# The low part of every fourth half piece of weights: from a subtraction on VectorE to an accumulating DMA

## The chip, the cores and the metric

The kernel runs on one core of a Trainium2 chip. The metric is the time of one execution on the device in microseconds (us). The engines are called TensorE (PE in the profile; PEld is its loading of stationary operands), VectorE (DVE), ScalarE (ACT), GpSimd (POOL) and SyncE (SP), which issues most of the DMAs.

## What is computed

Two transformer blocks follow each other on 256 tokens of 1024 columns, all in float32:

```
x = first_block(x, ...)        # u = rms_norm(h); z = u @ w_in; block-wise attention beside a gated
                               # recurrence; h += merged @ w_out;
                               # u = rms_norm(h); g, up = u @ w_gate_up; h += (silu(g) * up) @ w_down
for i in range(2):             # second block, two layers
    x += 0.5 * swiglu(rmsnorm(x, ffn1_norm[i]), w_gate, w_up, w_down)
    proj = rmsnorm(x, mix_norm[i]) @ w_in[i];  mkv = rmsnorm(mem, mem_norm[i]) @ w_mem_kv[i]
    x += concat([self_attention, memory_attention]) @ w_out[i]
    x += 0.5 * swiglu(rmsnorm(x, ffn2_norm[i]), w_gate, w_up, w_down)
```

## The kernel before

All weights are one stream of 227 pieces of 128 x 2048 float32 numbers (1 MB each). `load_to` has SP load a piece into one of three `raw` buffers. A piece is two half pieces of 128 x 1024. `split_to` makes two float32r operands of each: ScalarE casts it to the high part `wh` (line 204) and VectorE subtracts this from the original to get the low part `wl` (line 205), 512 columns at a time. There are eight buffers for `wh` and eight for `wl`, so a half piece takes over the buffers of the one eight places before it in the stream, and both wait until TensorE has read that one for the last time. In the program a split is asked for four half pieces ahead of the use (`SPLIT_AHEAD`).

An activation, which is the stationary operand, is split in the same way (`uh`, `ul`; `hh`, `hl`), and a product is three matmuls (`mm3`): high by high, high activation by `wl`, low activation by `wh`. Each half piece is used twice, for the first 128 tokens (t = 0) and for the second (t = 1).

Five feed-forwards (`ffn_body`) make up most of the time. In step j of 11 the stages are `gu(0, j)`, `dn(0, j-1)`, `gu(1, j)`, `dn(1, j-1)`. A `gu` uses four half pieces, in 24 matmuls; a `dn` uses two, in 12. The result of a `gu` goes through a tanh on ScalarE (`th`, line 356) and two instructions on VectorE (lines 357 and 359, to `hid`), and then TensorE transposes it in the next stage but one (line 154, `trbank<-cst,hid`), after six of its matmuls. Norms use a power on GpSimd (`power`, line 261, to `r` and `fac`).

TensorE's order is written out by hand: `Order` keeps a clock and places the small products of attention and recurrence beside the stream. The order on the other engines is a list scheduler's; `crit()` raises the priority of what stands under it. Each engine runs its own list in order.

Of the kernel before, what the change touches and what calls it, by code (L numbers as in the profile page):

```python
# [13 lines left out]
ALU = mybir.AluOpType  # L14
# [16 lines left out]
# the second block's distances on the clock of Order, by layer and then by group of heads (MEM: the memory's) and half of  # L31
# the tokens: projection to normalised heads, scores to the next group's, scores to normalised probabilities
# [5 lines left out]
# columns of the constants  # L38
C_ID, C_INV = 0, 128
C_N = 160  # L40
# columns of the constants of the first block
D_TRI, D_ONE, D_COS, D_SIN, D_CAUS, D_MLM, D_CHK = 0, 128, 256, 384, 512, 640, 768
D_N = 896
# columns of the per-partition parameters
# [5 lines left out]
# columns of the parameters that lie along the free dimension  # L50
# [4 lines left out]
class Ready:  # L55
    """When the operands of a later product can be expected, on the clock of Order."""
# [5 lines left out]
class Order:  # L62
    """Places the work beside the stream of large products in TensorE's program order.

    A task is a generator that emits instructions and yields what it waits for: a distance on the clock, or a list of
    Ready. The clock advances by the cost of the products emitted.
    """
# [30 lines left out]
    def until(self, *events):  # L98
        """Lets tasks go on until the events are ready."""
        self.run()  # L100
        while self._due(events) > self.now:
            nxt = min([self._due(w) for _, w in self.tasks] + [self._due(events)])
            assert nxt < math.inf
            self.now = max(self.now, nxt)
            self.run()
# [8 lines left out]
def kernel(  # L114
# [66 lines left out]
    # ScalarE's tables are loaded before the first operands are there  # L181
# [25 lines left out]
    def split_to(n):  # L207
        """Splits the first n half pieces."""
        while stream["split"] < min(n, 2 * NP):
# [5 lines left out]
            for s in range(0, 1024, SPLIT_W):  # L215
                split(hi[:, s:s + SPLIT_W], lo[:, s:s + SPLIT_W], r[:, 1024 * m + s:1024 * m + s + SPLIT_W])
# [14 lines left out]
    def lin(u, pieces, k0=0):  # L231
        """[tokens, 512] = u @ the pieces, each of four k tiles by 512 columns."""
# [13 lines left out]
    def lin_both(us, pieces):  # L246
        """lin for both halves of the tokens, which take turns."""
# [15 lines left out]
    def row_rstd(src, prescale=None):  # L263
        """rstd of the rows of src, or of src times prescale."""
# [24 lines left out]
    def put_T(u, k0, n, src, gains=None, gain1=None, keep=None):  # L289
        """u[:, k0:k0+n] = the n blocks of 128 columns of src, transposed, times gains, in two parts."""  # L290
# [18 lines left out]
    def boundary(t, src, gains, wait=1.4, keep=None, after=None):  # L309
        """The transposed operand of the next products: src times gains."""  # L310
# [108 lines left out]
    def scores(mix, qT, kT, t, n, st, mask=None, bias=None):  # L419
        """Softmax numerators and sums of four heads; qT, kT: [128, 2 pairs, tokens].  # L420

        mask: an operand and its identity, added by TensorE to the last 128 keys; bias: [128, 4 heads, n].
        """
# [33 lines left out]
    def probs_T(dst, p, n):  # L457
        """dst = the transposed blocks of p, [128, heads, keys], by head and by block of keys."""
# [10 lines left out]
    def heads_out(u, k0, st, v):  # L469
        """u[:, k0:k0 + 2] = the transposed sums over keys of four heads, in two parts; v(kb, head): values."""  # L470
# [9 lines left out]
    # =========================== first block ===========================  # L480
    def first_mix(p0):
        with tc.tile_pool(name="mix1", bufs=1, reuse_waits="tile") as mix:
# [25 lines left out]
            # the input in transposed form, and the gates of the recurrence from it  # L508
            def chain(*parts):
                """A task of parts, each a function and the time after it."""  # L510
# [77 lines left out]
            # -- recurrence --  # L588
# [110 lines left out]
            # -- attention --  # L699
# [706 lines left out]
```

## Time and profile before

| | |
|---|---|
| time, median of 2 executions | 1406.24 us (1406.09 and 1406.39) |
| span of the profiled execution, first to last instruction | 1404.3 us |
| TensorE busy | 1384.1 us, 99% |
| VectorE busy | 921.4 us, 66% |
| ScalarE busy | 766.8 us, 55% |
| GpSimd busy | 57.8 us, 4% |
| granted TensorE clock | 1.000 (2.4 GHz) over the span |
| DMA | 246.59 MB, mean 176 GB/s |

The profiled execution's own time is not listed apart from the two times; the start and the end that lie around its span are the difference, about 1.9 us. Busy time leaves out the issuing of DMAs and waiting for semaphores. Matmuls overlap each other, so the rows give them some 0.39 us each while one starts every 0.23 us. In the stretch of the feed-forward that the rows show, from 294.3 on, one step takes 17.06 us.

### The profile page before, as it was taken

Reading aid. Unit: us, or ns where it says so; the run is one execution under the profiler, and the core shown is the slowest. Engines: PE = TensorE matmul, PEld = TensorE weight load, DVE = VectorE, ACT = ScalarE, POOL = GpSimd, SP = SyncE. Lnnn points to the kernel's source line nnn. Section 1 sums busy time; section 2 is a strip of 40 time slices with the busy share of each in tenths; the row PEclk is TensorE's granted clock in tenths of the full one; section 3 lists DMA queues with packets and bytes.
Section 4 is the critical chain, followed back from the end, with each engine's and each line's share of the span. In section 5 each row is a group of like instructions: output and inputs, shape, how many; then the busy total and the mean of one; then the engine's idle time right before and its main releaser. Section 6 shows DMA issues by size and latency. Waiting matters only on the chain.

```text
span 1404.3 us, 18083 instructions
## 1 busy us (share of the span) xinstructions
PE 1384.1 (99%) x6598; PEld 1124.1 (80%) x6598; DVE 921.4 (66%) x1839; ACT 766.8 (55%) x1577; POOL 57.8 (4%) x59
## 2 busy tenths in 40 slices
PE   8999999999999999999999999999999989999998
PEld 6777888888888888877888888888888767888887
DVE  7866587555585575768575665755756787755554
ACT  6556555444474454668565544644545567544442
POOL 0000000000010000022000000000000121000000
PEclk9999999999999999999999999999999999999999
DMA  7534546554546454554255555555454532455540
GB/s 293 180 122 149 180 144 240 191 192 183 180 171 220 180 180 180 175 196 155 91 184 192 194 186 196 210 189 195 166 203 155 182 121 96 172 185 196 191 180 30
DMA packets 37081, 246.59 MB, mean 176 GB/s; under 512 B 4736, under 2 KB 5760, under 8 KB 8064
## 3 DMA queue, kind: packets, MB, share of 16 engines
q1 hardware_dynamic: 35568, 243.09, 48.4%
q10 hardware_dynamic: 1424, 2.34, 0.5%
q8 instruction: 52, 0.85, 0.2%
q14 instruction: 37, 0.30, 0.1%
HBM read 244.37 MB, written 1.05 MB: 175 GB/s over the span
## 4 chain that ended last, share of the span: by engine, by line
PE 90%; DVE 6%; POOL 2%; ACT 1%; issue 1%; DMA 0%; SPq 0%; DVEq 0%; POOLq 0%; ACTq 0%
PE bank L149 86%; PE trbank L154 4%; POOL fac L261 2%; DVE wl L205 2%; DVE ms L942 1%; ACT p L443 1%; DVE nm L441 1%; DVE z L946 1%; DMA h<-in_x_dram 0%; DVE p L453 0%; DVE p L439 0%; DVE z L1004 0%; DVE p L1041 0%; DVE z L1006 0%; DVE z L1007 0%
## 5 line engine op out<-in xcount | busy, mean ns | idle before, releaser
L205 DVE TENSOR_TENSOR wl<-raw,wh 128x512 fp32r<-128x512 f32 x908 | 583.7, 687 | 193.1 <-ACT wh L204 190.3
L204 ACT CAST wh<-raw 128x512 fp32r<-128x512 f32 x908 | 518.2, 619 | 238.4 <-PE bank L149 228.8
L149 PE MATMUL bank<-wh,uh 128*128 128x512 f32 x1248 | 505.8, 405 | 0.0
L149 PE MATMUL bank<-wh,ul 128*128 128x512 f32 x1248 | 490.4, 393 | 0.0
L149 PE MATMUL bank<-wl,uh 128*128 128x512 f32 x1248 | 487.5, 391 | 0.0
L149 PEld LDWEIGHTS bank<-wh,ul 128*128 128x128 f32 x1248 | 234.5, 188 | 52.8
L149 PEld LDWEIGHTS bank<-wl,uh 128*128 128x128 f32 x1248 | 235.3, 189 | 44.7 <-DVE wl L205 0.3
L149 PEld LDWEIGHTS bank<-wh,uh 128*128 128x128 f32 x1248 | 235.1, 188 | 44.6 <-issue 1.9
L149 PE MATMUL bank<-wh,hh 128*128 128x512 f32 x440 | 173.0, 393 | 0.0
L149 PE MATMUL bank<-wl,hh 128*128 128x512 f32 x440 | 172.4, 392 | 0.0
L149 PE MATMUL bank<-wh,hl 128*128 128x512 f32 x440 | 172.4, 392 | 0.0
L356 ACT ACTIVATE th<-bank,rs 128x256 f32<-128x256 f32 x110 | 52.2, 475 | 189.1 <-PE bank L149 188.8
L357 DVE SCALAR_TENSOR_TENSOR th<-th,bank 128x256 f32<-128x256 f32 x110 | 46.3, 421 | 166.3 <-ACT th L356 166.3
L149 PEld LDWEIGHTS bank<-wl,hh 128*128 128x128 f32 x440 | 82.7, 188 | 18.3
L149 PEld LDWEIGHTS bank<-wh,hl 128*128 128x128 f32 x440 | 82.6, 188 | 18.0
L149 PEld LDWEIGHTS bank<-wh,hh 128*128 128x128 f32 x440 | 82.8, 188 | 17.5
L204 ACT CAST hh<-trbank 128x256 fp32r<-128x256 f32 x110 | 40.6, 369 | 49.9 <-PE trbank L154 49.9
L261 POOL TENSOR_TENSOR r<-ms,mhalf 128x1 f32<-128x1 f32 x22 | 18.4, 837 | 908.9 <-DVE ms L271 908.9
L359 DVE SCALAR_TENSOR_TENSOR hid<-bank,rs,th 128x256 f32<-128x256 f32 x110 | 53.2, 484 | 3.5
L205 DVE TENSOR_TENSOR hl<-trbank,hh 128x256 fp32r<-128x256 f32 x110 | 46.1, 419 | 10.4 <-ACT hh L204 10.3
L261 POOL TENSOR_TENSOR fac<-ms,mhalf 128x4 f32<-128x4 f32 (+2 forms) x26 | 38.1, 1464 | 246.6 <-DVE ms L943 139.1
L154 PEld LDWEIGHTS trbank<-cst,hid 128*128 128x128 f32 x220 | 30.4, 139 | 14.6
(223 smaller groups left out, 947.2 us busy)
## 6 DMA issues: line engine op xcount, KB each, us to landing
raw<-in_weights_dram SPq DMA_DIRECT2D x226, 1024.0 KB, 4.9
mem<-in_mem_dram ACTq DMA_DIRECT2D x4, 512.0 KB, 4.5
Tb<-in_rel_dram SPq DMA_DIRECT2D x3, 512.0 KB, 5.9
h<-in_x_dram SPq DMA_DIRECT2D x4, 256.0 KB, 3.9
raw<-in_weights_dram SPq DMA_DIRECT2D x2, 512.0 KB, 7.1
gf<-in_rows_dram SPq DMA_DIRECT2D x1, 512.0 KB, 4.2
out_dram<-h SPq DMA_DIRECT2D x2, 256.0 KB, 2.0
out_dram<-h SPq DMA_DIRECT2D x4, 128.0 KB, 1.8
```

The costliest lines, as they stand in the source:

```text
L149: pe.matmul(out=out, lhsT=lhsT, rhs=rhs, start=start, stop=stop)
L154: pe.transpose(out=out, in_=in_, identity=ident if identity is None else identity)
L204: act.copy(out=hi, in_=src)
L205: dve.tensor_tensor(out=lo, in0=src, in1=hi.bitcast(F32), op=ALU.subtract)
L261: pool.tensor_tensor(out=dst, in0=src, in1=mhalf[:, 0:n], op=ALU.pow)
L356: act.activation(out=th, in_=acc[:, 0:256], func=AF.Tanh, scale=rh[t])
L357: dve.scalar_tensor_tensor(out=th, in0=th, scalar=1.0, in1=acc[:, 0:256], op0=ALU.add, op1=ALU.mult)
L359: dve.scalar_tensor_tensor(out=hd, in0=acc[:, 256:512], scalar=r2[t], in1=th, op0=ALU.mult, op1=ALU.mult)
L441: dve.tensor_reduce(out=nm, in_=s, axis=AX.X, op=ALU.max, negate=True)
L443: act.activation(out=p[:, j, a, 0:n], in_=s[:, j], func=AF.Exp, bias=nm[:, j:j + 1], accum_out=sums[:, j, a:a + 1])
L942: dve.tensor_reduce(out=ms, in_=sq, axis=AX.X, op=ALU.add)
L946: dve.tensor_tensor(out=v, in0=v, in1=fac.unsqueeze(2).to_broadcast([128, n, w]), op=ALU.mult)
```

## The change

From piece 8 on, every fourth half piece (the second half of each odd piece, 109 of 454) is split in another way. ScalarE writes the negated source, rounded to float32r, into `wl` in one instruction of 1024 columns; GpSimd issues a DMA that adds the source itself onto it, out of the same `raw` buffer; ScalarE casts the source to `wh` in one more instruction of 1024 columns. VectorE has no part in it. Comments are dropped elsewhere in the file, which moves line numbers by 7 behind this place (204 and 205 stay).

```diff
@@ split_to
             hi = wp.tile([128, 1024], FR, tag="wh", bufs=W_BUFS, name="wh")
             lo = wp.tile([128, 1024], FR, tag="wl", bufs=W_BUFS, name="wl")
-            for s in range(0, 1024, SPLIT_W):
-                split(hi[:, s:s + SPLIT_W], lo[:, s:s + SPLIT_W], r[:, 1024 * m + s:1024 * m + s + SPLIT_W])
+            if i >= 8 and (2 * i + m) % 4 == 3:
+
+                src = r[:, 1024 * m:1024 * m + 1024]
+                act.activation(out=lo, in_=src, func=AF.Copy, scale=-1.0)
+                pool.dma_start(out=lo, in_=src, accum_op=ALU.add)
+                act.copy(out=hi, in_=src)
+            else:
+                for s in range(0, 1024, SPLIT_W):
+                    split(hi[:, s:s + SPLIT_W], lo[:, s:s + SPLIT_W], r[:, 1024 * m + s:1024 * m + s + SPLIT_W])
```

In the whole program ScalarE has 690 casts of 128x512 and 109 of 128x1024 to `wh` where it had 908 of 128x512, and 109 negations of 128x1024; VectorE has 690 subtractions to `wl` where it had 908; GpSimd has 109 DMAs that it did not have. TensorE's order and SP's are the same.

The first place is ScalarE's list in the feed-forward of the first block, from the casts of a B0 on. Before, in the order of the list: casts of B0 (`raw_2744`), a tanh, B1 (the same piece), A0 and A1 of the step after (`raw_2775`), a transposed `hh`, the next tanh, A2 (`raw_2908`):

```order
L204 CAST wh_2910<-raw_2744 128x512 x2
L356 ACTIVATE th_2833<-bank_2801,rs_2137 128x256
L204 CAST wh_2929<-raw_2744 128x512 x2
L204 CAST wh_2943<-raw_2775 128x512 x2
L204 CAST wh_2955<-raw_2775 128x512 x2
L204 CAST hh_2922<-trbank_2924 128x256
L356 ACTIVATE th_2967<-bank_2907,rs_2096 128x256
L204 CAST wh_2974<-raw_2908 128x512
L204 CAST hh_3005<-trbank_3007 128x256
L204 CAST wh_2974<-raw_2908 128x512
```

Now, at the same place of the same engine (the buffers have other numbers; B1 and the A3 behind A2 are of the changed kind):

```order
L204 CAST wh_2890<-raw_2725 128x512 x2
L218 ACTIVATE wl_2910<-raw_2725 128x1024
L363 ACTIVATE th_2813<-bank_2781,rs_2124 128x256
L220 CAST wh_2909<-raw_2725 128x1024
L204 CAST wh_2922<-raw_2755 128x512 x2
L204 CAST wh_2934<-raw_2755 128x512 x2
L204 CAST hh_2902<-trbank_2904 128x256
L363 ACTIVATE th_2946<-bank_2887,rs_2083 128x256
L204 CAST wh_2953<-raw_2888 128x512
L204 CAST hh_2983<-trbank_2985 128x256
L204 CAST wh_2953<-raw_2888 128x512
L218 ACTIVATE wl_2966<-raw_2888 128x1024
```

B1's negation stands ahead of the tanh, its cast to `wh` behind it; the order of the rest is the same.

The second place is GpSimd's list in the attention of the second block's first layer. Before, it holds powers for the norms of the heads (`fac`) and the filling of a mask (`Tb`):

```order
L261 TENSOR_TENSOR fac_5720<-ms_5717,mhalf 128x8
L971 MEMSET Tb 64x4x64
L261 TENSOR_TENSOR fac_5793<-ms_5790,mhalf 128x8
L971 MEMSET Tb 64x4x64
L261 TENSOR_TENSOR fac_5880<-ms_5877,mhalf 128x8
L261 TENSOR_TENSOR fac_5984<-ms_5981,mhalf 128x8
L261 TENSOR_TENSOR fac_6073<-ms_6070,mhalf 128x4
L261 TENSOR_TENSOR fac_6173<-ms_6170,mhalf 128x4
```

Now, from the same power on:

```order
L268 TENSOR_TENSOR fac_5672<-ms_5669,mhalf 128x8
L219 DMA wl<-raw 128x1024
L268 TENSOR_TENSOR fac_5745<-ms_5742,mhalf 128x8
L978 MEMSET Tb 64x4x64
L268 TENSOR_TENSOR fac_5831<-ms_5828,mhalf 128x8
L219 DMA wl<-raw 128x1024
L268 TENSOR_TENSOR fac_5935<-ms_5932,mhalf 128x8
L268 TENSOR_TENSOR fac_6023<-ms_6020,mhalf 128x4
L219 DMA wl<-raw 128x1024
L268 TENSOR_TENSOR fac_6123<-ms_6120,mhalf 128x4
```

A DMA, which waits for ScalarE's negation, stands ahead of a power there three times, and one of the two fillings has moved ahead of this stretch.

## Rows read from the trace of the kernel before

**Rows 1.** Stretches: us, busy us (instructions) by engine, clock, DMA share, GB/s.

```profile
594.00:720.00 126.00, 122.90 (x687) 98.39 (x685) 91.23 (x200) 85.36 (x206) 17.93 (x16) 1.00 0.44 156
1091.00:1225.00 134.00, 125.98 (x671) 99.45 (x670) 101.50 (x218) 87.08 (x213) 21.00 (x16) 1.00 0.39 138
...
sum 1404.30, PE 1384.09 PEld 1124.08 DVE 921.37 ACT 766.75 POOL 57.79; mean PE 92.27 PEld 74.94 DVE 61.42 ACT 51.12 POOL 3.85
```

**Rows 2.** The chain that ended last, shares of the span by line.

```profile
by line: PE bank L149 85.9%; PE trbank L154 4.0%; POOL fac L261 1.9%; DVE wl L205 1.8%; issue 0.7%; DVE ms L942 0.6%; ACT p L443 0.6%; DVE nm L441 0.5%; DVE z L946 0.5%; DMA h<-in_x_dram 0.4%; DVE p L453 0.4%; DVE p L439 0.4%; DVE z L1004 0
```

**Rows 3.** Groups by line: busy us, mean ns of one, idle us before and releaser.

```profile
L205 DVE TENSOR_TENSOR wl<-raw,wh 128x512 fp32r<-128x512 f32 x908 | 583.7, 687 | 193.1 <-ACT wh L204 190.3
L204 ACT CAST wh<-raw 128x512 fp32r<-128x512 f32 x908 | 518.2, 619 | 238.4 <-PE bank L149 228.8 <-DMA raw<-in_weights_dram 4.5 <-ACT wh L204 3.0
...
L267 ACT ACTIVATE junk<-h 128x1024 f32<-128x1024 f32 x18 | 19.0, 1058 | 24.2 <-DVE h L1186 19.8 <-DMA h<-in_x_dram 2.5 <-DVE h L391 1.5
```

**Rows 4.** One step of the first block's feed-forward, as a stretch (columns: PE, PEld, DVE, ACT, POOL).

```profile
294.30:311.36 17.06, 17.06 (x78) 13.89 (x77) 9.89 (x20) 8.28 (x17) 0.00 (x0) 1.00 0.51 185
```

**Rows 5.** Timeline of TensorE in feed-forwards: start us, us, instruction.

```profile
303.52 0.39 PE L149 MATMUL bank<-wl,uh 128*128 128x512 f32 x1
...
306.26 0.39 PE L149 MATMUL bank<-wl,uh 128*128 128x512 f32 x1
...
310.67 0.37 PEld L154 LDWEIGHTS trbank<-cst,hid 128*128 128x128 f32 x2
...
314.10 0.39 PE L149 MATMUL bank<-wl,uh 128*128 128x512 f32 x1
...
316.88 0.40 PE L149 MATMUL bank<-wl,hh 128*128 128x512 f32 x1
...
1374.52 0.39 PE L149 MATMUL bank<-wl,uh 128*128 128x512 f32 x1
...
1385.04 0.39 PE L149 MATMUL bank<-wl,hh 128*128 128x512 f32 x1
```

**Rows 6.** Waits of TensorE: us in total, times, longest us.

```profile
PE trbank L154 <- DVE z L1007: 4.2, 3, 2.7
...
PE trbank L154 <- DVE p L1041: 2.2, 1, 2.2
```

**Rows 7.** Timeline of ScalarE, then VectorE, in the same step: start us, us.

```profile
302.62 0.62 ACT L204 CAST wh<-raw 128x512 fp32r<-128x512 f32 x1 [3.76 <-PE bank L149]
...
303.41 0.62 ACT L204 CAST wh<-raw 128x512 fp32r<-128x512 f32 x1
...
305.54 1.14 ACT L204 CAST wh<-raw 128x512 fp32r<-128x512 f32 x2 [0.17 <-PE bank L149]
306.92 0.47 ACT L356 ACTIVATE th<-bank,rs 128x256 f32<-128x256 f32 x1 [0.23 <-PE bank L149]
...
303.28 0.69 DVE L205 TENSOR_TENSOR wl<-raw,wh 128x512 fp32r<-128x512 f32 x1 [3.44 <-ACT wh L204]
...
307.42 0.42 DVE L357 SCALAR_TENSOR_TENSOR th<-th,bank 128x256 f32<-128x256 f32 x1
307.88 0.48 DVE L359 SCALAR_TENSOR_TENSOR hid<-bank,rs,th 128x256 f32<-128x256 f32 x1
...
311.89 0.42 DVE L205 TENSOR_TENSOR hl<-trbank,hh 128x256 fp32r<-128x256 f32 x1
```

**Rows 8.** GpSimd's power of four columns by form; landing of the 512 KB `mem` loads.

```profile
L261 POOL TENSOR_TENSOR fac<-ms,mhalf 128x4 f32<-128x4 f32 x12 | 14.3, 1188 | 165.5 <-DVE ms L657 107.5 <-DVE ms L943 58.1
...
DMA to landing us min/median/max: 3.8/4.5/5.9
```

**Rows 9.** `raw` loads from 294 to 330: one issue, GB/s in 40 slices, landing.

```profile
309.59 0.33 SPq L199 DMA_DIRECT2D raw<-in_weights_dram  x1
...
GB/s 255 428 437 419 410 255 0 0 0 0 0 0 0 0 91 173 419 437 209 218 419 437 382 428 291 18 0 0 0 0 0 0 0 109 228 410 382 127 273 428
...
DMA to landing us min/median/max: 4.8/5.1/6.3
```

## The prediction

> **What bounds the kernel now.** I read the busy times first. TensorE is busy for 1384.09 of 1404.30 us, VectorE for 921.37, ScalarE for 766.75, GpSimd for 57.79 [rows 1]. The chain of waits agrees: 85.9% of the time that decides the end is TensorE's products into `bank`, and only 1.8% is the subtraction that makes `wl` [rows 2]. Then I read where TensorE stands still at all, in the same table of stretches [rows 1]. Of its 20.2 us, 3.10 lie in the first attention of the second block (594 to 720) and 8.02 in the second one (1091 to 1225); the other 9.1 lie before the first operands are there and behind the last product. In a feed-forward it is 0.00 [rows 4]. So the work of VectorE, from which the change takes 218 instructions, is not what anybody waits for in most of the program. TensorE in its turn is waited for: ScalarE's casts to `wh` stand for 228.8 us on TensorE [rows 3], since a half piece gets its buffers only when the half piece eight before it has been used for the last time. That distance is the time a split may take.
>
> **How long a split may take.** In a feed-forward the step is 17.06 us long, with TensorE busy all through [rows 4]. Call the half pieces of a step A0 to A3 (gate and up) and B0, B1 (down). Each is used for the first half of the tokens and then for the second, in the order A0-A3, B0, B1, A0-A3, B0, B1. So A3 takes the buffer of the A1 before and B1 that of the A3 before. On TensorE's rows [rows 5] the old low part is last read at 303.52 + 0.39 = 303.91 for A3's buffer and first read anew at 314.10: 10.19 us. For B1's buffer it is 306.26 + 0.39 = 306.65 and 316.88: 10.23 us. In the later feed-forwards the step is shorter: 1374.52 + 0.39 = 1374.91 and 1385.04 for the last tight one, 10.13 us. Pairing all 109 changed half pieces like this on TensorE's rows, 46 have 10.1 to 10.4 us, 5 have 10.7 to 11.1, 4 have 13 to 14, and 54 have 14.6 us or more (an A1 takes over a B1's buffer, 18.8 to 19.0). The low part of today's split needs two casts and two subtractions, about 2 us of this.
>
> **The change, part by part.** (1) VectorE loses 218 subtractions of 583.7 / 908 = 0.643 us [rows 3], 140 us in all. Nothing of it lies on the path in the feed-forwards, where TensorE never waits. In the two attention stretches TensorE waits 11.12 us in all, the longest of it for results of VectorE (4.2 and 2.2 us [rows 6]). Those 11 us are the most that the relief can give: -0.8%, 1395. I count nothing, because ScalarE, on the same chains, gets slower there.
> (2) ScalarE trades 218 casts of 518.2 / 908 = 0.571 us for 218 instructions of 1024 columns, for which the nearest row is the squaring of 128x1024, 1.058 us [rows 3]: 230.6 - 124.5 = +106 us, 873 us in all, or 62%. In a feed-forward step it goes from 8.28 to at most 10.2 of 17.06 us [rows 4], hidden behind TensorE. Where the negation now stands ahead of the tanh (`th`), as in the first order listing, that tanh starts at about 306.65 + 0.04 + 1.06 = 307.75 and not at 306.92, 0.8 us late. The hidden values (ready at 308.36 [rows 7]) are flipped by TensorE after six products of the next stage, from 310.67 on [rows 5]: 2.3 us of slack, 1.5 left. Cost: nothing.
> (3) The low part gets a new chain: release, ScalarE's negation, GpSimd's issue, the transfer, TensorE. Release to ScalarE is 0.04 us (a hop from ScalarE to VectorE, 306.92 + 0.47 = 307.39 to 307.42, is as short [rows 7]), the negation 1.06, the hop to GpSimd 0.04. ScalarE is free at both moments: the casts ahead of A3's end at 304.03, those ahead of B1's at 306.68 [rows 7]. So of 10.13 us there remain 10.13 - 1.14 = 9.0 us for the transfer D, from GpSimd's issue to its landing. No row shows a transfer out of SBUF into SBUF, nor one that adds. Bounds: it moves 512 KB, and the quickest 512 KB load of this trace lands after 3.8 us [rows 8]. It has to read 512 KB of `raw` and 512 KB of `wl`, as much as a `raw` load of 1024 KB, which lands after 4.8, 5.1 or 6.3 us (least, median, most) in this stretch [rows 9]. If reading and adding were two passes one after the other, it would be 10.2 us. On top comes GpSimd's issue, of which there is no row either; I take the row of its 4-column power, 1.19 us [rows 8]. I take the load of the same reading: D = 5.1 + 1.2 = 6.3 us for A3, whose transfer starts at 305.2 into an idle queue. For B1, which starts at 307.9 in the middle of the `raw` loads, I take the slowest of these: 6.3 + 1.2 = 7.5 us. The queue shows the difference: it is empty for some 7 us of each step and busy at over 400 GB/s for the rest [rows 9]. Both are under 9.0, by 2.7 and 1.5 us. Cost: nothing. The range of D is 3.8 to 10.2 + 1.2 = 11.4.
> (4) The raw buffer is held until the transfer has landed, and SP, which issues in order, waits with the next load and all behind it. B1's load goes out at 307.85 + 7.5 = 315.4 instead of 309.59 [rows 9] and lands 6.3 us later, at 321.7. Its first cast is at 305.54 + 17.06 = 322.60 [rows 7], and even if it were late, that half piece has 10 us for a split of 2. A3's load goes out at 311.5, and its first cast comes one step after 302.62 [rows 7], at 319.7. Cost: nothing; it starts to cost at a D of about 15.
> (5) GpSimd runs 109 issues in its one queue, mixed with the powers (second listing). An issue waits there for ScalarE's negation, and a power behind it feeds the head norms, whose wait is in the chain with 1.9% [rows 2]. There are 11 issues in the two attention stretches. If each held up a power on the path by its own 1.19 us and one negation of 1.06, that would be 25 us. GpSimd stands idle for 165.5 us before the 12 powers of four columns alone [rows 8], and those stretches have 13 us and more for a low part, so I count nothing and keep up to 10 us for the range.
> Sum: 1404.3 + 0 us of span. The execution with its start and end takes 1.9 us more (1406.24 timed, against the span of 1404.3), so **1406 us**.
>
> The Trainium skill, DMA: Bandwidth & Descriptors (Latency and other measured facts), gives 1 us to the first byte of a DMA issued from GpSimd and 0.6 us from SP. No run here shows it yet; an estimate by that page would be a D of 5.1 + 0.4 = 5.5 us, and the sum would be the same.
>
> **The rivals.** *The adding transfer is slow (slower).* D counts only beyond 9.0 us, and then at each of the 46 + 5 tight half pieces. At two passes, D = 11.4: 46 x 2.4 + 5 x 1.7 = 119 us, 1525 us. 2% (28 us) is reached at D = 9.6, where 46 x 0.6 = 28. For it: nothing in the trace shows an add inside a transfer, and all tight ones are in stretches without any slack of TensorE. Against it: the queue is half empty, and the loads run at over 400 GB/s.
> *GpSimd cannot issue while VectorE works (slower).* If writing the transfer's orders had to wait for a gap of VectorE, it would wait for the end of its run, which goes from 303.28 almost without a gap to 312.31 [rows 7]. The change shortens that run by 1.3 us per changed half piece, to about 309.6 (with an A3 and an A1) or 310.9 (with a B1). Then A3 lands at 309.6 + 6.3 = 315.9, 1.8 us late, and B1 at 310.9 + 7.5 = 318.4, 1.5 us late: 51 x 1.65 = 84 us, 1490 us. The Trainium skill, SBUF — State Buffer (SBUF: two separate sides), describes such a lock, but for copies and the like on VectorE in a faster mode, and says of the two-input subtraction that it has no such mode; by that the run here would not lock anything, and no row here shows it either way. I give it little.
> *The relief counts (faster, within 2%).* If the shorter queue of VectorE took away all waits in the attention stretches, 1406 - 11 = 1395 us. Against it: ScalarE stands on the same chains and takes 8 x 2 x (1.058 - 0.571) = 8 us more in each.
> *The change does not relieve what it names.* VectorE's 140 us do go, but it was idle for 34% already: this is the forecast itself.
>
> **How the numbers follow.** Forecast (no cost above 10 us): 0.54. Relief counts: 0.09, 1395 to 1402. Slow adding transfer: 0.26, 1434 to 1530. Locked issue: 0.06, around 1490. A gain of over 2% has no mechanism here; I leave 0.03 for what I do not see, and 0.02 for slower by something else. About 2% is what a measurement of this kernel can tell from no change. So slower 0.34, same 0.63, faster 0.03. The range begins at 1395. Above, it must take in about half of the slow cases to leave out no more than 2 in 10; with D between 9.6 and 11.4 they spread from 1434 to 1525, so I end it at 1500. Likeliest case alone: 1396 to 1416.
>
> **What would show it.** In the profile of the changed kernel: 690 subtractions of `wl` on VectorE instead of 908; GpSimd's transfers with a median to landing of 6 to 8 us; no line in which TensorE waits for a transfer into `wl`; TensorE without idle time in the feed-forwards and steps of 17.06 us. The forecast is wrong if that landing is above 9 us: then TensorE's waits name the DMA into `wl` at A3 and B1 about 50 times, the steps come out longer in pairs, and the A1s still wait for nothing. If GpSimd's issue comes late behind runs of VectorE, its lock is right; if the waits are in the attention stretches only, GpSimd's queue is.

## Result and the profile after

| | before | after |
|---|---|---|
| time, median | 1406.24 us | 1425.74 us (1424.02 and 1427.47) |
| ratio | | 1.0135, 95% interval 1.0112 to 1.0158 |
| profiled execution: time, span | | 1427.47, 1425.7 us |

The changed kernel is slower by 1.35%, 19 us. That is outside the 1396 to 1416 us of the likeliest case, inside the range, and below 2%. Two executions of the versions below stand far from all others, 2310.8 us in E4 and 3563.7 us in E5, and are left out of the ratios, though not of the medians.

The page's busy times, whole span (engine, busy us, share, instructions):

```profile
PE 1391.5 (98%) x6598; PEld 1124.4 (79%) x6598; DVE 797.1 (56%) x1621; ACT 846.4 (59%) x1577; POOL 149.0 (10%) x168
```

VectorE has lost 124 us of work and ScalarE has got 80, as the edit says. TensorE runs the same 6598 matmuls and is busy for 7.4 us more, at a mean granted clock of 0.996 instead of 1.000; the other 14 us of the span's 21.4 are time in which it stands. The three stretches that answer to [rows 1] and [rows 4], moved to where the same work lies now:

```profile
599.70:731.40 131.70, 124.30 (x686) 98.89 (x685) 81.42 (x183) 92.55 (x207) 24.99 (x25) 0.99 0.60 181
1107.40:1244.20 136.80, 128.12 (x671) 100.31 (x670) 92.98 (x200) 93.35 (x211) 28.21 (x25) 0.99 0.56 165
296.70:313.76 17.06, 17.06 (x77) 13.86 (x76) 7.54 (x14) 8.74 (x17) 1.72 (x2) 1.00 0.85 258
```

The feed-forward step is as it was, 17.06 us without a gap, with the DMA engines busy for 0.85 of it instead of 0.51. The first attention has grown by 5.7 us, 4.3 of them idle. Groups by line, which answer to [rows 3]:

```profile
L205 DVE TENSOR_TENSOR wl<-raw,wh 128x512 fp32r<-128x512 f32 x690 | 449.0, 687 | 277.7 <-ACT wh L204 275.3
L204 ACT CAST wh<-raw 128x512 fp32r<-128x512 f32 x690 | 393.5, 618 | 241.4 <-PE bank L149 212.4 <-DMA raw<-in_weights_dram 26.8 <-ACT wh L204 0.9
...
L218 ACT ACTIVATE wl<-raw 128x1024 fp32r<-128x1024 f32 x109 | 115.5, 1059 | 1.3 <-PE bank L149 1.0
L220 ACT CAST wh<-raw 128x1024 fp32r<-128x1024 f32 x109 | 113.6, 1042 | 4.9 <-PE bank L149 4.9
L219 POOL DMA_DIRECT2D wl<-raw x109 | 95.2, 873 | 1023.0 <-ACT wl L218 875.3 <-ACT hh L204 133.1 <-PE bank L149 8.1
```

What is new on a cast is the last but one cause: ScalarE stands 26.8 us for `raw` loads, where it was 4.5. The DMA issues (count, KB, median us to landing), the landing of all transfers into `wl`, and SP's waits:

```profile
raw<-in_weights_dram SPq DMA_DIRECT2D x226, 1024.0 KB, 5.2
wl<-raw POOLq DMA_DIRECT2D x109, 512.0 KB, 6.8
mem<-in_mem_dram ACTq DMA_DIRECT2D x4, 512.0 KB, 8.2
Tb<-in_rel_dram SPq DMA_DIRECT2D x3, 512.0 KB, 8.4
...
DMA to landing us min/median/max: 4.5/6.8/11.4
...
SPq L199 <- DMA wl<-raw: 1005.3, 108, 12.8
```

TensorE's waits (us in total, times, longest) name a transfer into `wl` for 2.7 us only; the others are for results of VectorE and ScalarE:

```profile
PE trbank L154 <- DVE p L460: 5.2, 2, 4.6
...
PE trbank L154 <- DVE hid L366: 2.9, 2, 2.7
PE bank L149 <- DMA wl<-raw: 2.7, 5, 0.6
PE bank L149 <- ACT qkT L1024: 2.6, 1, 2.6
PE trbank L154 <- DVE h L871: 2.5, 1, 2.5
```

**Where the time went.** The 5448 matmuls on weights come in the same order in both kernels, so I read for each how far it starts behind its twin. From there the loss can be dated. The times are those of the kernel before. A jump is a delay that comes at one place and stays. The changed execution is 1.8 us ahead before any of it, by a shorter wait for the first load, which is no effect of the change; so the stretches sum to 23.2 us where the spans differ by 21.4.

```
191-235  +4.0   one jump of 3.0 at 202.9, then 0.9 at a clock of 0.96
235-594  +3.5   0.8 at 420.9 and 454.7 (low part of a B1 late), 1.2 at 588.3
594-720  +5.8   one jump of 5.1 at 628.5
720-901  +4.0   2.9 at 726.2, 0.6 at 881.4 (a B1)
901-1091 +1.0   0.9 at 1084.5
1091-1225 +2.8  several, up to 2.7, both ways
1225-end +2.1   0.8 at 1249.8 and 0.6 at 1283.6 (B1s)
```

So the loss is a sum of few events at a block's start or end and in attention, beside some B1s. Each version has one profile, and the sizes vary from one to the next: the wait for the B1 at 420.9 is 0.8 us here, 2.3 in E4 and 2.9 in E8. Three events were followed back. At 628.5, on GpSimd, VectorE and TensorE:

```profile
633.76 0.30 POOL L978 MEMSET Tb<- 64x256 f32 x1 [5.01 <-DMA Tb<-in_rel_dram]
634.03 1.63 POOL L268 TENSOR_TENSOR fac<-ms,mhalf 128x8 f32<-128x8 f32 x1
...
635.69 0.69 DVE L953 TENSOR_TENSOR z<-z,fac 128x512 f32<-128x512 f32 x1 [4.10 <-POOL fac L268]
...
636.94 1.09 PE L154 MATMUL trbank<-cst,p 128*128 128x128 f32 x4 [4.61 <-DVE p L460]
```

The filling of `Tb` now stands ahead of this power in GpSimd's list (before, it came behind it) and waits for `Tb`'s load; the power, the heads' norm on VectorE and the probabilities behind that in VectorE's list wait with it. At 726.2, on ScalarE, then TensorE:

```profile
736.53 0.62 ACT L204 CAST wh<-raw 128x512 fp32r<-128x512 f32 x1 [4.75 <-DMA raw<-in_weights_dram]
...
740.38 0.41 PE L154 MATMUL trbank<-cst,hid 128*128 128x128 f32 x2 [2.73 <-DVE hid L366]
```

After the border ScalarE splits several half pieces in a row and comes to one whose `raw` load is late, and the tanh behind it in its list is late too. SP's issue of that load, and its time to landing:

```profile
725.91 0.33 SPq L199 DMA_DIRECT2D raw<-in_weights_dram  x1
...
DMA to landing us min/median/max: 10.5/10.5/10.5
```

It goes out 2.4 us later than its twin, when a transfer that held its buffer has landed, and is then under way for 10.5 us beside the next transfer, where the twin took 5.1. So of this delay 2.4 us come from the held buffer and 5.5 from the slower landing in company. At 202.9, on VectorE, then TensorE:

```profile
202.16 0.29 DVE L900 TENSOR_TENSOR lp<-gr 128x128 f32<-128x128 f32 x1 [1.91 <-DMA gr<-in_rows_dram]
...
203.42 1.11 PE L154 MATMUL trbank<-cst,h 128*128 128x128 f32 x4 [2.47 <-DVE h L871]
```

A small load (8.0 us to landing instead of 6.7, and issued 3.0 us later than its twin) holds up VectorE's list, in which the residual `h` stands behind it. Not followed back are the 1.2 us at 588.3 and the 0.9 at 1084.5, where TensorE waits at a block's end for a low part `hl` from VectorE.

### The profile page after: what moved, and what is told of

The parts are those of the page before. It is cut to its first block, busy times and chain, and to the rows that moved or that the text cites. A ratio compares the mean times of both kernels' runs of the same rounds, so it can differ in the third digit from the quotient of the medians.

```text
span 1425.7 us, 18279 instructions
## 1 busy us (share of the span) xinstructions
PE 1391.5 (98%) x6598; PEld 1124.4 (79%) x6598; DVE 797.1 (56%) x1621; ACT 846.4 (59%) x1577; POOL 149.0 (10%) x168
## 3 DMA queue, kind: packets, MB, share of 16 engines
q0 software_dynamic: 15696, 57.15, 20.6%
## 4 chain that ended last, share of the span: by engine, by line
PE 40%; DMA 4%; DVE 4%; ACT 3%; issue 2%; POOL 2%; POOLq 0%; DVEq 0%; ACTq 0%
PE bank L149 38%; DMA wl<-raw 3%; PE trbank L154 2%; DMA raw<-in_weights_dram 2%; POOL fac L268 1%; DVE wl L205 1%; ACT wl L218 1%; ACT wh L204 1%; ACT p L450 1%; DVE z L953 0%; DVE ms L949 0%; DVE nm L448 0%; DVE z L1011 0%; DVE z L1013 0%; DVE p L446 0%
## 5 line engine op out<-in xcount | busy, mean ns | idle before, releaser
L205 DVE TENSOR_TENSOR wl<-raw,wh 128x512 fp32r<-128x512 f32 x690 | 449.0, 687 | 277.7 <-ACT wh L204 275.3
L204 ACT CAST wh<-raw 128x512 fp32r<-128x512 f32 x690 | 393.5, 618 | 241.4 <-PE bank L149 212.4
L219 POOL DMA_DIRECT2D wl<-raw x109 | 95.2, 873 | 1023.0 <-ACT wl L218 875.3
L220 ACT CAST wh<-raw 128x1024 fp32r<-128x1024 f32 x109 | 113.6, 1042 | 4.9 <-PE bank L149 4.9
L218 ACT ACTIVATE wl<-raw 128x1024 fp32r<-128x1024 f32 x109 | 115.5, 1059 | 1.3 <-PE bank L149 1.0
```

The source lines that it names most:

```text
L204: act.copy(out=hi, in_=src)
L205: dve.tensor_tensor(out=lo, in0=src, in1=hi.bitcast(F32), op=ALU.subtract)
L218: act.activation(out=lo, in_=src, func=AF.Copy, scale=-1.0)
L219: pool.dma_start(out=lo, in_=src, accum_op=ALU.add)
L220: act.copy(out=hi, in_=src)
```

## Experiments

Each is timed against the kernel before on the same chip; differences in us are the ratio times 1406. Each version gets new lists from the scheduler, so an edit can also change the order on an engine that it does not name. **First theory (H):** the held raw buffers delay all loads, and these delays are the loss. **Rivals:** the low part is late or the lists are too long (L); the DMA engines are short of capacity (C).

**E1, nothing held.** The transfer reads the weights in DRAM:

```diff
-                pool.dma_start(out=lo, in_=src, accum_op=ALU.add)
+                pool.dma_start(out=lo, in_=weights[i, :, 1024 * m:1024 * m + 1024], accum_op=ALU.add)
```

> The accumulating transfer reads the same values of the half piece from the weights in DRAM instead of from the raw buffer, so that a raw buffer is free once ScalarE has negated and cast it; the negations, the casts, the 109 issues on GpSimd and the lateness of the low part stay. Theory H (the changed kernel loses its 19.5 us because the transfer holds the raw buffer, and SP's loads, taken in order, come late): SP's 1005 us of waits for the transfer are gone, ScalarE's 26.8 us of waits for raw loads fall back to about 4.5, the jumps of 5.1, 3.0 and 2.9 us are gone, and what stays is the direct waits of about 4 us: 1407 to 1413 us. Rival L (the low part is late, or ScalarE's or GpSimd's list is too long): 1420 to 1428, as in the changed kernel. Rival C (the DMA engines are short of capacity): not better, 1425 or more, since 57 MB more come from DRAM.

Measured: 1442.65 us, 1.0256 (1.0240 to 1.0272). ScalarE no longer waits for `raw` loads (1.0 us in all) and the jumps at 628.5 and 726.2 are gone, as H says, but the one at 202.9 stays (3.0), and the total is 17 us worse than the changed kernel, which is C's sign. The loads now run beside the transfers, and these become late themselves:

```profile
raw<-in_weights_dram SPq DMA_DIRECT2D x226, 1024.0 KB, 7.3
wl<-in_weights_dram POOLq DMA_DIRECT2D x109, 512.0 KB, 8.1
...
PE bank L149 <- DMA wl<-in_weights_dram: 17.2, 5, 5.0
```

Two of the jumps say nothing for or against H. At 628.5 the filling of `Tb` stands behind the power again in this version's list of GpSimd, and at 202.9 VectorE's list stands for another small load, `pi`, which SP does not issue:

```profile
642.26 1.64 POOL L268 TENSOR_TENSOR fac<-ms,mhalf 128x8 f32<-128x8 f32 x1 [3.07 <-DVE ms L950]
647.77 0.31 POOL L978 MEMSET Tb<- 64x256 f32 x1 [3.88 <-DMA Tb<-in_rel_dram]
...
200.53 0.17 DVE L897 CAST pf<-pi 128x2 f32<-128x2 int32 x1 [6.95 <-DMA pi<-in_positions_dram]
```

H is not the whole story. Loads may be slower here because no held buffer keeps them apart from the transfers, or because 57 MB more come from DRAM; E1 does not tell these two apart.

**E2, holding alone.** The kernel before, and beside each of the 109 splits a plain copy out of the raw buffer:

```diff
+            if i >= 8 and (2 * i + m) % 4 == 3:
+                spare = wp.tile([128, 1024], F32, tag="spare", bufs=1, name="spare")
+                pool.dma_start(out=spare, in_=r[:, 1024 * m:1024 * m + 1024])
```

> The kernel before, with all low parts from VectorE, and beside it a plain copy of the same 109 half pieces by a DMA of GpSimd's queue from the raw buffer into a spare tile that nobody reads. It holds the raw buffer and loads the DMA engines as the change does; no low part is late and ScalarE's list is as before. Theory H: a good part of the 19.5 us is here, 1414 to 1424 us, with ScalarE's waits for raw loads at 15 us or more. Rival L: 1406 to 1408. Rival C: as H, but with ScalarE's waits there even if nothing holds the buffers.

Measured: 1412.12 us, 1.0041 (1.0027 to 1.0055), +5.8. Between H and L; ScalarE waits 4.6 us for `raw` loads, not 15, and SP waits only 196.6 us for the copies: a copy needs the load alone and starts before ScalarE and VectorE have read the buffer, so the buffers were held for less time than meant. The largest jump is the one at 202.9 (1.5 us), with `gr` landing after 9.4 us.

**E3, ScalarE's part alone.** No transfer; VectorE subtracts 1024 columns:

```diff
                 act.activation(out=lo, in_=src, func=AF.Copy, scale=-1.0)
-                pool.dma_start(out=lo, in_=src, accum_op=ALU.add)
                 act.copy(out=hi, in_=src)
+                dve.tensor_tensor(out=lo, in0=src, in1=hi.bitcast(F32), op=ALU.subtract)
```

> The changed kernel without the transfer: for the 109 half pieces ScalarE's negation and 1024-wide cast stay, and VectorE writes the low part in one 1024-wide subtraction. What is left is ScalarE's 109 more operations of 1.06 us and its longer steps. Theory H: 1405 to 1409 us, no more than 3 us from before. Rival L in the form that ScalarE's list is too long: 1412 or more.

Measured: 1413.78 us, 1.0050 (1.0036 to 1.0064), +7.0: more than H's 1405 to 1409 allows, and in the range of L, 1412 or more. Most of it came in the attention stretches, at a granted clock of 0.97 in 1091 to 1225. In this execution the clock fell to 0.50 (1.2 GHz) three times in attention, each time behind a wait of TensorE of 1.95 to 2.18 us, and TensorE fell 1.6, 1.6 and 1.0 us further behind its twin meanwhile; some of this it won back where the twin waits.

**E4, small loads on another queue.** The loads of `gr` and `Tb` from ScalarE's queue:

```diff
-            nc.sync.dma_start(out=Tb[c], in_=rel[:, 4 * c:4 * c + 4])
+            nc.scalar.dma_start(out=Tb[c], in_=rel[:, 4 * c:4 * c + 4])
```

> The changed kernel with the four small loads that stand among the weights in SP's list (gr once, Tb three times) issued from ScalarE's queue instead, where they wait behind no raw load. Theory H: the jumps at 203 and 628.5 us (3.0 and 0.9 at the lower clock, 5.1) go, the rest stays: 1415 to 1419 us. If these jumps come from GpSimd's list (transfers ahead of the powers) or from slow DMA engines alone: 1423 to 1428.

Measured: 1428.13 us, 1.0149 (1.0131 to 1.0166): no better. The jump at 202.9 fell to 0.9 (in E8 below, which leaves `gr` alone, it is 1.1, so this says little), but the one at 628.5 was there again (5.08), with the MEMSET waiting as before:

```profile
637.13 0.30 POOL L978 MEMSET Tb<- 64x256 f32 x1 [5.09 <-DMA Tb<-in_rel_dram]
637.40 1.63 POOL L268 TENSOR_TENSOR fac<-ms,mhalf 128x8 f32<-128x8 f32 x1
```

SP's queue is not the cause there. At 1428.13 instead of H's 1415 to 1419, H falls as the single cause. **Second theory (S):** a sum of events, each where a list taken in order meets a late row.

**E5 and E6, by place.** The change in the feed-forwards' pieces only (82 half pieces), and in the attention stages' only (27):

```diff
-            if i >= 8 and (2 * i + m) % 4 == 3:
+            if (30 <= i < 96 or 112 <= i < 178 or 194 <= i) and (2 * i + m) % 4 == 3:      # E5
+            if (8 <= i < 30 or 96 <= i < 112 or 178 <= i < 194) and (2 * i + m) % 4 == 3:  # E6
```

> The change only in the feed-forward pieces (30 to 95, 112 to 177, 194 to 226): 82 of the 109 half pieces; in the attention stages all low parts come from VectorE. New theory S (the loss is a sum of small ones: about 5 us where a product of the feed-forward has a lead of only 10.1 to 10.2 us and the transfer takes 8.4 or more, about 5 us at block borders, and the rest in the attention stages, where lists of ScalarE, VectorE and GpSimd that are taken in order get a row in another place): 1412 to 1417 us; no jump at 203, 628 and 1150. Theory H (one queue of loads that is always late): at least three quarters of the loss stay, 1420 or more.

> The complement: the change only in the attention pieces (8 to 29, 96 to 111, 178 to 193), 27 half pieces. Theory S: 1415 to 1420 us, with the jumps at 203 (3.0 and 0.9) and 628.5 (5.1) there and none in the feed-forward; with the run before this one it makes up the whole loss. Theory H: a quarter of it, 1409 to 1411.

Measured: 1416.09 us, 1.0057 (1.0042 to 1.0071), +8.0, and 1415.78 us, 1.0059 (1.0046 to 1.0073), +8.3. S: a quarter of the transfers makes nearly half of the loss, and E6 has the jumps at 202.9 (1.9) and 628.5 (4.2), which E5 has not. Together 16.3 of the 19 us; each of the two is uncertain by 2 us. TensorE's waits in E5:

```profile
PE bank L149 <- DMA wl<-raw: 4.0, 6, 1.4
```

These six, which are jumps of 5.0 us in all, are direct waits for the low part of a B1 whose transfer landed 9.1 to 9.8 us after its issue: five in the first steps of a block, one at its end.

**E7, long leads only.** 85 half pieces of the feed-forwards whose products come 16.5 us or more after their buffer is free. In the prediction's names these are A1 of every step and A0 of every second one (the expectation calls that piece the down projection's, which is wrong; it is the first one of gate and up). In the list of first pieces 96 - 33 is 63 once more:

```diff
+            j = next((2 * (i - a) + m for a in (30, 63, 112, 145, 194, 96 - 33) if a <= i < a + 33), 0)
+            if j % 6 == 5 or j % 12 == 4:
```

> The change in 85 half pieces of the feed-forward, all of them those whose products come 16.5 us or more after their buffer is free (both halves of the down projection's piece, one of them every second step), where the run with 82 has two in three at 10.1 to 10.2 us. As many transfers, negations and held raw buffers. Theory S: the direct waits go, 1406 to 1411 us. Theory H: the same as with the 82, whatever that is.

Measured: 1422.65 us, 1.0112 (1.0097 to 1.0127), +15.8. A miss: the direct waits are gone, yet it costs twice E5. The large jumps are now all near a block's start, where TensorE waits for `hid`: 2.8 at 228, 1.2 at 432, 4.4 at 726, 0.9 at 914, 3.3 at 1230. ScalarE's row at the first of them, TensorE's sum, and ScalarE's:

```profile
225.88 0.62 ACT L204 CAST wh<-raw 128x512 fp32r<-128x512 f32 x1 [4.66 <-DMA raw<-in_weights_dram]
...
PE trbank L154 <- DVE hid L367: 11.6, 5, 4.2
...
ACT wh L204 <- DMA raw<-in_weights_dram: 23.4, 10, 6.2
```

The load that ScalarE waits for at 225.88 went out right behind the landing of a transfer that took 10.2 us, and landed 4.8 us after its issue, where the median before is 4.9: here the held buffer makes the delay.

**E8, the filling waits for nothing.** `Tb` loaded in two parts that leave out the corner that GpSimd fills:

```diff
-            nc.sync.dma_start(out=Tb[c], in_=rel[:, 4 * c:4 * c + 4])
+            nc.sync.dma_start(out=Tb[c][0:64, :, 0:192], in_=rel[0:64, 4 * c:4 * c + 4, 0:192])
+            nc.sync.dma_start(out=Tb[c][64:128], in_=rel[64:128, 4 * c:4 * c + 4])
```

> The changed kernel with each load of Tb in two parts that leave out the corner which GpSimd's MEMSET fills, so that the MEMSET waits for no load and cannot hold up the power behind it. Theory S: the jump of 5.1 us at 628.5 is gone and the rest stays, 1418 to 1422 us. If VectorE waited there for another reason: 1424 to 1428.

Measured: 1421.70 us, 1.0104 (1.0088 to 1.0119), 4.4 us better than the changed kernel, whose interval (1.0112 to 1.0158) it just overlaps. As S says, the jump at 628.5 is gone:

```profile
628.62 0.30 POOL L979 MEMSET Tb<- 64x256 f32 x1
631.99 1.64 POOL L268 TENSOR_TENSOR fac<-ms,mhalf 128x8 f32<-128x8 f32 x1 [3.07 <-DVE ms L950]
...
633.66 0.69 DVE L953 TENSOR_TENSOR z<-z,fac 128x512 f32<-128x512 f32 x1 [1.81 <-POOL fac L268]
...
634.91 0.82 PE L154 MATMUL trbank<-cst,p 128*128 128x128 f32 x4 [0.51 <-DVE p L460]
```

The lists of the other versions agree: where the filling stands ahead of this power and waits for its load (the changed kernel, E4, E6) the jump is 5.1, 5.1 and 4.2 us, and where it stands behind it (E1, E2, E3, E12) it is 0.6 us or nothing.

**Third theory (B)** for E7: at a block's start ScalarE works off several half pieces in a row and needs the loads one after the other; there a held buffer delays it.

**E9, E10, E11: what E7's loss is.** E7 with the transfer from DRAM as in E1; E7 without the transfer as in E3; E7 in the middle eight steps of each block only, that is half pieces 12 to 59 of its 66 (60 changed ones; the expectation calls these the steps 2 to 9):

```diff
-            if j % 6 == 5 or j % 12 == 4:
+            if 12 <= j < 60 and (j % 6 == 5 or j % 12 == 4):      # E11
```

> The kernel with the 85 half pieces of long lead (it lost 16 us), with the accumulating transfer reading the same values from the weights in DRAM, so that it holds no raw buffer. Theory B (its loss is the held buffer at a block's start, where ScalarE catches up and needs loads one after the other): the jumps of 2.8, 4.4 and 3.3 us at 228, 726 and 1230 us go with ScalarE's 23.4 us of waits for raw loads, 1406 to 1411 us. If ScalarE's longer list makes them: 1418 or more.

> The same 85 half pieces without the transfer: ScalarE negates and casts 1024 columns, VectorE writes the low part in one subtraction. Theory B: ScalarE's part costs little in the feed-forward, 1406 to 1410 us. If ScalarE's longer list at the block's start is the cause: 1414 or more.

> As the kernel with 85 half pieces of long lead, with the transfer from the raw buffer, but only in the steps 2 to 9 of the eleven of each feed-forward block: 60 half pieces, none near a block's start or end. Theory B: no cost that can be measured, 1405 to 1408 us. If a held raw buffer costs wherever it is: 60/85 of the 16 us, 1415 or more.

Measured: E9 1415.19 us, 1.0069 (1.0052 to 1.0086); E10 1407.84 us, 1.0006 (0.9996 to 1.0017); E11 1406.05 us, 0.9996 (0.9988 to 1.0005). E10 and E11 are as B says: without the transfer there is no loss, and with transfer and held buffer away from the borders there is none either. E9 lies between B's range, 1406 to 1411, and its rival's. It confirms B in its place (the jumps at 228, 726 and 1230 are gone or under 1 us, and ScalarE's waits for `raw` are down from 23.4 to 3.1 us) and shows another: 4.8 us at 432 and 2.1 at 914, where the memory's load goes out. ScalarE's list stands for it:

```profile
430.85 1.06 ACT L275 ACTIVATE junk<-mem 128x1024 f32<-128x1024 f32 x1 [9.83 <-DMA mem<-in_mem_dram]
...
DMA to landing us min/median/max: 3.5/9.5/11.6
```

The second row is the landing of the `mem` loads, 4.5 us before [rows 8]. No buffer is held here; the DMA engines are shared, and more comes from DRAM. In the changed kernel, which reads nothing more from DRAM, the same loads land after 8.2 us. So theory C has its place too.

**E12, attention without the transfer.** E6 with E3's edit.

> The change in the 27 half pieces of the attention stages (it lost 9 us) without the transfer: the negation, the 1024-wide cast and one subtraction on VectorE. Theory S: the jumps at 203 and 628.5 us, which a late load and GpSimd's list make, are gone; ScalarE's 27 us in lists that the scores and softmaxes share cost 3 to 7 us, 1409 to 1413 us. If the transfer makes all of the 9 us: 1406 to 1408.

Measured: 1409.99 us, 1.0023 (1.0014 to 1.0031), +3.2, as S says, without jumps at 202.9 and 628.5. Of E6's 8.3 us, ScalarE's longer list makes 3.2 and the transfer, with what it does to GpSimd's list, the other 5.

**E13, E14, E15: is a lead of 10.1 us too short?** The middle eight steps only, in the prediction's names: A3 and B1 in turn (40); A3 and B1 of every step (80); the changed kernel's own turn of A3, A1, B1 (60):

```diff
+            if 12 <= j < 60 and (2 * i + m) % 4 == 3 and j % 6 != 5:   # E13
+            if 12 <= j < 60 and j % 6 in (1, 3):                       # E14
+            if 12 <= j < 60 and (2 * i + m) % 4 == 3:                  # E15
```

> The 40 half pieces of the changed kernel's choice that lie in the steps 2 to 9 of a feed-forward block and have a lead of only 10.1 to 10.2 us (the first of the two halves of the up projection's second piece's kind and of the other, in turn). No block border, no attention. If the direct wait for a late transfer is a term of its own: three to six jumps of 0.6 to 1.6 us, 1409 to 1413 us. If such waits come only where a border or an attention stage has upset the lists before: 1405 to 1408, as with the long leads.

> The same steps with a transfer in both places of every step, 80 half pieces with a lead of 10.1 to 10.2 us. If 8 to 9.5 us from issue to landing against a lead of about 9 after the negation is the limit, twice the transfers share the DMA engines and more of them pass it: at least twice the cost of the 40, 1413 to 1425 us. If the lead is enough: 1405 to 1409.

> The changed kernel's own choice in the steps 2 to 9 of each feed-forward block: the 40 half pieces of short lead, which cost nothing alone, and the 20 of long lead between them, 60 in all. If the third one in the turn moves the raw loads into the time of the others' transfers (in the changed kernel the second kind of short lead takes 8.2 us from issue to landing beside 7.1 us of raw loads, with the 40 alone 5.7 us beside 3.2): 8 us again, slack near 0 and some direct waits, 1408 to 1411 us. If only borders and attention upset the turn: 5 to 6 us, no waits, 1405 to 1407.5.

Measured: E13 1406.46 us, 0.9995 (0.9986 to 1.0004); E14 1406.91 us, 1.0005 (0.9995 to 1.0014); E15 1408.80 us, 1.0011 (1.0000 to 1.0023). So a lead of 10.1 us is enough by itself. For each transfer I read D, from issue to landing, what is left until its first product, and how long `raw` loads were on their way beside it (summed over loads):

```
                    D min/median/max   left min/median   beside raw loads
after   A3 (27)       4.5/4.6/10.7        2.6/4.2             1.9
after   B1 (28)       4.5/8.2/9.5         0.04/0.53           7.1
after   A1 (27)       5.6/9.4/11.4        3.7/6.8            11.1
E13     A3 (20)       4.5/4.5/5.7         3.0/4.2             0.0
E13     B1 (20)       5.4/5.7/6.7         2.1/3.0             3.2
E14     B1 (40)       4.9/5.3/6.9         1.2/2.8             4.0
E15     B1 (20)       5.4/8.3/9.1         0.04/0.46           7.2
E15     A1 (20)       9.1/9.4/10.3        5.8/6.9            10.8
```

The same B1s land after 5.7 us in E13 and 8.3 in E15, which has the A1s between them. The A1s' held buffers move the `raw` loads into the B1s' time. Twice as many transfers (E14) do no harm if the loads lie elsewhere (its profiled execution is its slowest of twelve, 1411.03 us, by a jump of 2.5 at 914). In E15 the slack is all but used up, and the loss is about 1.5 us, at the edge of the noise (0 to 3.2); ScalarE waits 22 times for `raw` loads there, 22.0 us in all, and TensorE waits for none of its results. The changed kernel's cost in the middle of the blocks is thus about 1.5 us for 60 half pieces, and by difference the 22 nearer to a border add 6.5 in E5. Four of E5's six direct waits (248.7, 454.7, 746.2, 780.0) are at B1s that E15 has too and does not wait for: the transfers at the border make those behind them late.

## Why the prediction was wrong

The forecast was no cost. Of the terms put at nothing, four cost something at blocks' borders or in attention: ScalarE's list in (2), a B1's transfer in (3), the late loads in (4), GpSimd's list in (5). By its terms:

(1) **VectorE's relief is worth nothing: right.** It lost 124 us of work, where the text had 140, and with 60 half pieces taken off it and nothing upset (E11) the time is 0.9996.

(2) **ScalarE's longer list is hidden: right in the feed-forwards** (E10: 0.0006, which is not to be told from nothing), **wrong in attention**: 3.2 us for 27 half pieces (E12). The text had named 8 us more work in each of these stretches and then set it off against the relief. ScalarE got 80 us of work in all, not 106.

(3) **D is 6.3 us for A3 and 7.5 for B1, limit 9.0, "Cost: nothing": right for A3, and for B1 this step failed near the borders.** Measured 4.6 and 8.2 (medians). The estimate for A3 was too high, since the issue takes 0.86 and not 1.19 us and the reading of 1024 KB is no measure of it; for B1 too low, since it was taken from loads that had the DMA engines to themselves, and a B1's transfer takes 5.7 us beside 3.2 us of loads and 8.3 beside 7.2. The mechanism, a cost only beyond 9.0, was right: a few B1s pass it (up to 9.5), which gives five jumps of 0.6 to 0.8 us, about 3.6 in all here, and 5.0 in E5. The estimate by the Trainium skill (DMA: Bandwidth & Descriptors, Latency and other measured facts), 5.5 us, lies between the two medians and takes no account of company.

(4) **"The raw buffer is held ... Cost: nothing; it starts to cost at a D of about 15": this step failed.** It was worked out in one steady step, and there it holds (E11, E13, E14: no cost). At a block's start ScalarE catches up and every `raw` load is on the path: E7 loses 15.8 us there with D at a median of 6.8, and only 0.8 without the transfer (E10). In the changed kernel itself this is the one jump of 2.9 at 726.2. "All behind it" was named and not priced: the small load of `gr` stands in that queue, and its jump is 3.0. And the transfers slow the loads by sharing the DMA engines, held or not (`mem` 8.2 us instead of 4.5, E9 9.5), which no term had.

(5) **GpSimd's list, "I count nothing and keep up to 10 us": this failed with 4.4 us** (E8). Not the issues held up the power, as the text had it, but the filling of `Tb`, which the scheduler had moved ahead of it. The second order listing shows that move; the text looked at the issues only. It also counted 11 issues in the two attention stretches, where the rows show 18 (GpSimd's 25 instructions instead of 16 in each), so that its own worst case would have been some 40 us and not 25.

**Its signs, and the range.** The 690 subtractions and the median of 6.8 us to landing came as written; that TensorE waits for no transfer into `wl` did not. The sign for being wrong, a landing above 9 us, did not come either: the loss came at a median below it. That 1425.74 lies in the range is luck: most of the room above 1416 was left for the slow transfer of the first rival, which did not come.

**The rivals.** The slow adding transfer is wrong as priced: D is not 11.4 us but 4.6 and 8.2, and there are 5 waits and not 50; what is left of it are the B1s. GpSimd locked out by VectorE is wrong: an issue takes 0.87 us in the mean, and nearly all its waits name ScalarE. The relief does not count. The last sentence of the prediction (waits in attention only: GpSimd's queue) came nearest, for 4.4 of the 19 us.

**The sum.** In the changed kernel's own execution 5.1 us are the filling, 3.6 the late B1s, 3.0 the jump behind `gr` and 2.9 the one behind the late load at 726.2. The other 8.6 of the 23.2 us are smaller steps: in attention, at the ends of blocks, and at TensorE's lower clock behind the jump at 202.9. The timed versions agree as far as their noise lets them: E5's +8.0 and E6's +8.3 make 16.3 of 19, and the 2.7 left are within it. Within E6, 3.2 are ScalarE's list (E12) and about 4.4 the filling (E8); the 0.7 left for `gr` is less than its jump of 1.9 there. Within E5, 5.0 are direct waits for B1s by its trace. Open is how the other late loads divide between held buffers and shared DMA engines (at 726.2 it is 2.4 to 5.5 us, in E7 at 228 all of it the held buffer), and what makes the 1.2 us at 588.3 and the 0.9 at 1084.5. E3 loses 7.0 us where its attention part, E12, loses 3.2. By their traces 1.6 us of the difference lie in 235 to 594 (most of it at 408, where E10 has a delay too), 0.6 in the first attention and 1.8 in the second, where E3's clock fell twice and E12's once; what the clock makes of it is not separated. None of the versions beats the kernel before; the best (E11, E13) equal it.

## What to carry to other kernels

A transfer that holds its source buffer has to be priced where the consumer of the next load catches up, at a block's start, and not in the steady step, and together with the loads that are under way beside it; in the steady step it can be free even 80 times. Where the order of a list changes, price every row that now stands ahead of a row on the path, also those that the change did not add: here one MEMSET cost 4.4 us, about as much as all late low parts. The same holds for an experiment: E1 lost the jump at 628.5 by another order of a list, and not by what its edit was meant to test. Taking work off an engine that nobody waits for gave nothing, while ScalarE's longer list and GpSimd's new order cost something in attention, where slack was short.

## What the runs showed of the hardware

An accumulating transfer out of SBUF takes twice the DMA engines' time of a plain copy of the same 57.15 MB (E2): the DMA queue's lines, of the changed kernel, then of E2 (packets, MB, share of 16 engines):

```profile
q0 software_dynamic: 15696, 57.15, 20.6%
```

```profile
q0 software_dynamic: 15696, 57.15, 10.3%
...
spare<-raw POOLq DMA_DIRECT2D x109, 512.0 KB, 4.4
```

Left alone (E13's A3s) it still lands as soon, after 4.5 us against the copy's 4.4. Beside 7 to 11 us of `raw` loads it takes 8 to 9 us (B1 and A1 in the table above), and from DRAM (E1) the share is no less:

```profile
q0 software_dynamic: 15696, 57.15, 21.9%
```

TensorE's granted clock, 1.00 of 2.4 GHz in 191 to 235 before, was 0.96 there, so part of the time at the lower level of 1.2 GHz. The rows after the stop of 2.47 us at 203 show when:

```profile
204.76 0.63 PE L149 MATMUL bank<-wl,uh 128*128 128x512 f32 x1
...
206.78 0.39 PE L149 MATMUL bank<-wh,uh 128*128 128x512 f32 x1
```

For some 2 us a matmul took 0.63 us instead of 0.39.
